# Batch norm behind a matmul: ten column units of the weight multiplied in strips of 32 columns

## The chip, the cores and the metric

The kernel runs on one core of a Trainium2 chip. TensorE multiplies: a weight load puts a stationary operand into its array, and a matmul then moves rows of the other operand past it, into a bank of PSUM. VectorE (DVE), ScalarE (ACT) and GpSimd (POOL) work on tiles in SBUF and PSUM; SyncE (SP) issues most of the stores. The time is that of one execution on the device in microseconds. Before the change it is 208.61 us, the median of two runs (208.1 and 209.12).

## The reference

```
batch, m, k, n = 16, 512, 1024, 768
y = np.matmul(x, weight)                       # x: (16, 512, 1024), weight: (1024, 768)
mean = np.mean(y, axis=(0, 1), keepdims=True)
var = np.var(y, axis=(0, 1), keepdims=True)
y_norm = (y - mean) / np.sqrt(var + eps)
return gamma * y_norm + beta
```

All is float32 outside; gamma is ones, beta zeros, eps 1e-5. The mean and the variance of a column are taken over all 8192 rows, so no column of the output can be written before its last row has been multiplied.

## The kernel before

The 8192 rows of x are cut into 16 chunks of 512 (index `c`), the 768 columns of the weight into 6 tiles of 128 (index `nt`). The contraction of 1024 runs in 8 steps of 128: four values of `jw`, two of `e`. x and the weight are cast to bf16 as they are loaded. A chunk of x is transposed by DVE into `xT_sb`. In most chunks two neighbouring values of the contraction stay side by side there, so a matmul reads its rows with a stride of two elements; in the chunks 2, 3 and 6 (`SINGLE`) they are apart. For the chunks 4, 5 and 7 to 10 (`PARTED`), and later 11 to 15 (`LATE`), a copy by ACT, POOL or DVE makes plain rows of them (`x_pl`).

The tiles 0 and 1 are multiplied with x stationary (`mm_rows`) while x is loaded. The tiles 2 to 5 follow with w stationary, one tile after the other: a *column unit* (`col_unit`, emitted by `mm`) is one tile and one chunk. It takes 8 pairs of a 128x128 weight load and a matmul of 512 moving rows, which all add up in one PSUM bank (128 columns of w as partitions, 512 rows of x as its row). A unit comes in two halves of 4 pairs (`halves`). Behind its second half `col_stats` takes the statistics of the bank (DVE, or ACT in the chunks 4 to 15 of tile 2) and ACT keeps the values as bf16 in `y_sb`. When a tile has all its 16 chunks, its scale and shift are worked out, its kept values are normalized, turned back and stored, while TensorE is at the next tile. The last tile has nothing behind it: its normalization, turning (`o_ps`, `o_sb`, L1028 and L1293) and stores make the end of the program. Turns of earlier tiles by TensorE can be taken in between the matmuls of a unit (`todo`).

The order on every engine is made by a planner (`arrange`): each piece of work is a `Task` with a due time, a cost for each engine that can do it, and what it needs. The planner knows a column unit by the cost that `col_unit` gives it (1.728 us for plain rows, 1.808 us for strided ones), not by the instructions that it emits.

Names that the prediction uses: L558 is the matmul of a column unit; L736 the units of the last chunk of the last tile, in two pieces of 256 rows; L493 the matmuls with x stationary (256 moving); L798 those of the last two chunks for the tiles 0 and 1 (256 moving); L577 a row of small matmuls at the start (128 moving); L855 eight passes in f32 with one row moving, that sum statistics over partitions; L1028 the turns of the end (128 moving). PSUM has 8 banks, taken in turn by all of these.

Of the kernel before, what the change touches and what calls it, by code (L numbers as in the profile page):

```python
# [227 lines left out]
def kernel(  # L228
# [9 lines left out]
    nc = tc.nc  # L238
# [9 lines left out]
    P = 128  # L248
    NT = N // P
    KQ = K // 4  # L250
    CH = 512
    RT = CH // P
    C = M // CH
    QR = 256
    QPC = CH // QR
    JW = KQ // 64
# [3 lines left out]
    SMALL = 22  # L260
    TOUCH = 1
    EARLY = 4
    SHORT = 2
    GA = 2
    NA = GA * P
# [4 lines left out]
    RC = C - 2  # L270
    XT, YB, SQ = C - EARLY, 28, 3
    ADDED = (0,6,16,28,40)
# [18 lines left out]
    def seq(bi):  # L291

        ins = bi.ins
        prev = last.get(ins.engine)
        if prev is not None:
            tc.add_manual_dep(
                ins, prev,
                mybir.DependencyInfo(mybir.DependencyClass.NoSync, mybir.DependencyReason.DATA),
                reason="order",
            )  # L300
        last[ins.engine] = ins.name
        return bi
# [7 lines left out]
    w_sb = singles.tile([P, JW, 2, N], bf16)  # L310
# [49 lines left out]
    def act(occ):  # L360
        return {"ACT": (occ, occ + 0.11)}
# [64 lines left out]
    order = [("x", 0), ("w", 0, 1)] + [("x", 1), ("w", 1, 2), ("w", 2, 4)]  # L426
    order += [("x", q) for q in range(2, SHORT * QPC)] + [("c", c) for c in range(SHORT, C - 1)]
    at = M - CH
# [5 lines left out]
    for kind, n, *n1 in order:  # L434
# [9 lines left out]
        rows = n1[0] if kind == "p" else QR if kind == "x" else CH  # L444
# [11 lines left out]
        for i in range(rows // QR):  # L456
            c, q = divmod(m0 // QR + i, QPC)
# [9 lines left out]
        if rows % QR:  # L467
            t0 = rows // QR * QR // 32
            m1 = m0 + 32 * t0
            c, q = divmod(m1 // QR, QPC)  # L470
# [8 lines left out]
    def x_of(c, jw, e, r0, r1):  # L479
        if c in SINGLE:  # L480
            return x_slot[c].tile[:, jw, e, r0:r1]
        return x_slot[c].tile[:, jw, r0:r1, e]
# [28 lines left out]
    def part_chunk(c, now, engines, small=False, step=0.0, after=()):  # L511

        src = x_slot[c]
        slots = [Slot(sqs if jw < SQ else ys) for jw in range(JW)] if small else [Slot(xts)] * JW
        ts = []

        def copy(jw):
            def emit(eng):
                if small:
                    if jw < SQ:  # L520
                        x_pl = sqpool.tile([P, 2, CH], bf16, tag="sq")
                    else:
                        x_pl = ypool.tile([P, 2, CH], bf16, tag="y")
                    slots[jw].tile = [x_pl]
                elif jw == 0:
                    x_pl = xtpool.tile([P, JW, 2, CH], bf16, tag="xT")
                    slots[0].tile = [x_pl[:, i] for i in range(JW)]
                dst = slots[jw].tile[0 if small else jw]
                pairs = src.tile[:, jw].rearrange("p m e -> p e m")
                seq(nc.scalar.copy(dst, pairs) if eng == "ACT" else ENG[eng].tensor_copy(dst, pairs))  # L530
            return emit

        for jw in range(JW):
            new = small or jw == 0
            ts.append(task(
                now + step * jw, engines, copy(jw), [x_ready[c, q, JW] for q in range(QPC)] + list(after) + ([] if new else ts[:1]),
                len(engines) > 1, uses=[src] + ([] if new else [slots[jw]]), takes=[slots[jw]] if new else []))
        plain[c] = slots, ts, small

    def moving(c, jw, e, r0, r1, parted):  # L540
        if parted:
            slots, _, small = parted
            return slots[jw].tile[0 if small else jw][:, e, r0:r1]
        return x_of(c, jw, e, r0, r1)

    def mm(nt, c, jws, slot, q0=0, q1=QPC):
        parted = plain.get(c)

        def emit(eng):
            if jws[0] == 0 and q0 == 0:  # L550
                y_ps = psum.tile([P, CH], f32, tag="b")
                slot.tile = y_ps
            y_ps = slot.tile[:, q0 * QR:q1 * QR]
            me = emit.task
            todo = [u for u, n in me.hosted for _ in range(n)]
            for jw in jws:
                for e in range(2):
                    seq(nc.tensor.matmul(  # L558
                        y_ps, w_sb[:, jw, e, nt * P:(nt + 1) * P],
                        moving(c, jw, e, q0 * QR, q1 * QR, parted),  # L560
                        start=(jw == 0 and e == 0 and q0 == 0), stop=(jw == JW - 1 and e == 1),
                        skip_group_check=True,
                    ))
                    if todo:
                        todo.pop(0).emit.step()
            while todo:
                todo.pop(0).emit.step()
        return emit
# [253 lines left out]
    for c in range(1, RC):  # L822
        for ts in ([0, 1], [2, 3]):
            rows_unit(c, ts)
        if c in PARTED:
            part_chunk(c, clock[0] + (4.0 if c < EARLY else 20.0), act(1.05))
        columns = ([c - 1] if 0 < c - 1 < EARLY and c - 1 in PARTED else []) + (
            [c] if c < EARLY and c not in PARTED else [])
        for c1 in columns:
# [372 lines left out]
    STEP = {2: 1.9, 3: 2.3, 4: 2.3}  # L1202
    CHUNKS = {nt: list(range(EARLY, C)) for nt in range(GA, NT)}
    if LATE:
        late = [c for c in range(EARLY, C) if c in LATE or c + 1 - c % 2 * 2 in LATE]
        rest = [c for c in range(EARLY, C) if c not in late]
        CHUNKS[NT - 3], CHUNKS[NT - 2] = late + rest, rest + late
    for nt in range(GA, NT - 1):
# [8 lines left out]
        start = clock[0] + 3.0  # L1217
# [12 lines left out]
    nt = NT - 1  # L1230
# [113 lines left out]
```

## Time and profile before

| | |
|---|---|
| median of the runs | 208.61 us (208.1 to 209.12) |
| span of the profiled execution, first to last instruction | 206.5 us |
| TensorE matmul busy | 191.4 us, 1211 instructions |
| TensorE weight load busy | 116.3 us, 1226 instructions |
| DVE, ACT, POOL busy | 156.3, 139.8, 132.0 us |
| L558 with x plain (`x_pl`) | 256 matmuls, 60.5 us |
| L558 with `xT_sb` | 241 matmuls, 55.1 us |
| last matmul of the last unit (L736) | 188.6 us |
| last stores issued by SP | 191.6 to 201.9 us |
| stores of 512 KB, from issue to landing | 3.7 us, median |

Times in the profile are in us from the first instruction, unless marked ns. PE stands for TensorE's matmuls, PEld for its weight loads. "L558" is line 558 of the kernel. The page cuts the span into 40 slices and gives for each the busy share of an engine in tenths, 9 for 90% or more; PEclk is the clock that TensorE was granted, in tenths of its full speed. The recorded time of a matmul reaches from its start to the modelled end of its results, so matmuls that follow each other closely overlap in the record: their pace is read from the distance of their starts. The chain of waits goes back from the last instruction to whatever released it, and names what the end of the program really hung on.

### The profile page before, as it was taken

Reading aid. Unit: us, or ns where it says so; the run is one execution under the profiler, and the core shown is the slowest. Engines: PE = TensorE matmul, PEld = TensorE weight load, DVE = VectorE, ACT = ScalarE, POOL = GpSimd, SP = SyncE. Lnnn points to the kernel's source line nnn. Section 1 sums busy time; section 2 is a strip of 40 time slices with the busy share of each in tenths; the row PEclk is TensorE's granted clock in tenths of the full one; section 3 lists DMA queues with packets and bytes.
Section 4 is the critical chain, followed back from the end, with each engine's and each line's share of the span. In section 5 each row is a group of like instructions: output and inputs, shape, how many; then the busy total and the mean of one; then the engine's idle time right before and its main releaser. Section 6 shows DMA issues by size and latency. Waiting matters only on the chain.

```text
span 206.5 us, 3506 instructions
## 1 busy us (share of the span) xinstructions
PE 191.4 (93%) x1211; PEld 116.3 (56%) x1226; DVE 156.3 (76%) x238; ACT 139.8 (68%) x248; POOL 132.0 (64%) x148
## 2 busy tenths in 40 slices
PE   7998999999999999999999999999999999996900
PEld 3465564747488888777875444444444445553600
DVE  4220779999999999968989998977999648947900
ACT  2000560369989999998978767997376776866950
POOL 7877964877488999999304999599954440440000
PEclk9999999999999999999999999999999999999995
DMA  5999999999999999999676898999999999999898
GB/s 55 169 168 193 192 196 196 196 198 197 190 193 197 197 197 195 196 197 195 110 120 199 311 339 307 267 350 307 315 317 245 291 325 308 274 341 347 254 347 243
DMA packets 98497, 48.73 MB, mean 236 GB/s; under 512 B 24240, under 2 KB 97968, under 8 KB 98480
## 3 DMA queue, kind: packets, MB, share of 16 engines
q0 software_dynamic: 34688, 18.36, 65.1%
q1 hardware_dynamic: 63792, 30.16, 52.8%
q8 instruction: 9, 0.15, 0.3%
q14 instruction: 8, 0.07, 0.1%
HBM read 36.71 MB, written 25.17 MB: 300 GB/s over the span
## 4 chain that ended last, share of the span: by engine, by line
PE 82%; DMA 8%; ACT 3%; issue 1%; POOL 1%; DVE 1%; ACTq 0%; POOLq 0%
PE y_ps L558 51%; PE y_ps L493 23%; DMA ring<-in_x_dram 5%; PE y_ps L798 4%; ACT o_sb L1293 3%; DMA w_sb<-in_weight_dram 3%; PE o_ps L1028 2%; PE a_ps L887 1%; POOL ring L392 1%; PE y_ps L736 1%; PE o_ps L1058 0%; ACTq L1339 0%; PE tot_ps L855 0%; DVE fin L743 0%; ACT y_sb L746 0%
## 5 line engine op out<-in xcount | busy, mean ns | idle before, releaser
L558 PEld LDWEIGHTS <-w_sb 128*128 128x128 bf16 x512 | 49.7, 97 | 57.4
L558 PE MATMUL y_ps<-x_pl,w_sb 128*128 128x512 bf16 x256 | 60.5, 379 | 0.3
L392 POOL DMA_DIRECT2D ring<-in_x_dram x76 | 47.5, 630 | 13.0 <-DVE xT_sb L414 5.0
L558 PE MATMUL y_ps<-xT_sb,w_sb 128*128 128x512 bf16 (+1 forms) x241 | 55.1, 376 | 0.4
L493 PE MATMUL y_ps<-w_sb,xT_sb 128*128 128x256 bf16 x448 | 50.7, 273 | 0.6 <-DMA w_sb<-in_weight_dram 0.6
L493 PEld LDWEIGHTS <-xT_sb 128*128 128x128 bf16 x448 | 43.6, 98 | 8.3 <-issue 1.7
L421 DVE STREAM_TRANSPOSE xT_sb<-ring 128x1024 f32<-128x1024 f32 (+1 forms) x29 | 31.2, 1111 | 12.4 <-DMA ring<-in_x_dram 12.2
L694 DVE BATCH_NORM_STATS2 stats<-y_ps 128x6 f32<-128x512 f32 x46 | 30.9, 687 | 12.7 <-PE y_ps L558 12.5
L698 ACT CAST y_sb<-y_ps 128x512 bf16<-128x512 f32 x51 | 29.4, 590 | 14.5 <-DVE stats L694 12.4
L926 POOL TENSOR_TENSOR ring<-ring,sum 128x1024 f32<-128x1024 f32 (+1 forms) x11 | 23.7, 2193 | 14.6 <-DVE ring L921 14.5
L649 POOL TENSOR_TENSOR sum<-sum,sq_sb 128x512 f32<-128x512 f32 x21 | 26.9, 1281 | 3.2 <-ACT sq_sb L642 2.1
L642 ACT ACTIVATE sq_sb<-y_ps 128x512 f32<-128x512 f32 x28 | 16.3, 607 | 18.0 <-PE y_ps L493 17.1
L645 DVE TENSOR_TENSOR sum<-y_ps,sum 128x512 f32<-128x512 f32 x28 | 18.9, 675 | 9.1 <-ACT sq_sb L642 7.8
L530 ACT COPY x_pl<-xT_sb 128x1024 bf16<-128x1024 bf16 x24 | 24.4, 1052 | 1.7 <-DVE xT_sb L421 1.7
L655 ACT CAST y_sb<-y_ps 128x512 bf16<-128x512 f32 x28 | 16.0, 599 | 7.8 <-DVE sum L645 7.6
L530 POOL COPY x_pl<-xT_sb 128x1024 bf16<-128x1024 bf16 x15 | 16.1, 1108 | 8.0 <-DVE x_pl L530 5.2
L921 DVE TENSOR_TENSOR ring<-y_sb,a_ps 128x1024 f32<-128x1024 bf16 (+1 forms) x16 | 16.7, 1080 | 0.3 <-DMA out_dram<-ring 0.3
L1139 POOL TENSOR_TENSOR ring<-ring,sum 128x1024 f32<-128x1024 f32 x4 | 9.6, 2412 | 11.0 <-DVE ring L1135 11.0
L1193 ACT CAST ring<-ring 128x1024 f32<-128x1024 bf16 x15 | 15.7, 1049 | 1.0 <-DMA ring<-y_sb 1.0
L1028 PE MATMUL o_ps<-ident,y_sb 128*128 128x128 bf16 x104 | 14.2, 221 | 2.2 <-DVE y_sb L1280 2.0
L414 DVE STREAM_TRANSPOSE xT_sb<-ring 128x2048 bf16<-128x2048 bf16 x6 | 13.5, 2289 | 0.2 <-DMA ring<-in_x_dram 0.2
L574 PE MATMUL idle_ps<-idle_sb 128*128 128x512 f32 x20 | 11.2, 717 | 1.5 <-DVE idle_sb L314 1.5
(97 smaller groups left out, 155.0 us busy)
## 6 DMA issues: line engine op xcount, KB each, us to landing
out_dram<-ring SPq DMA_DIRECT2D x38, 512.0 KB, 3.7
ring<-in_x_dram POOLq DMA_DIRECT2D x52, 256.0 KB, 8.8
out_dram<-o_sb SPq DMA_DIRECT2D x6, 512.0 KB, 4.9
ring<-in_x_dram POOLq DMA_DIRECT2D x16, 128.0 KB, 5.3
out_dram<-ring SPq DMA_DIRECT2D x4, 256.0 KB, 3.0
w_sb<-in_weight_dram POOLq DMA_DIRECT2D x8, 96.0 KB, 5.1
w_sb<-in_weight_dram POOLq DMA_DIRECT2D x4, 192.0 KB, 5.9
ring<-in_x_dram POOLq DMA_DIRECT2D x4, 192.0 KB, 8.1
```

The lines of the kernel that those rows point to most:

```text
L392: bi = seq(nc.gpsimd.dma_start(x_bf[32 * i:32 * i + 32], src[:, :, KQ * i:KQ * (i + 1)]))
L421: seq(nc.vector.transpose(dst, src[:, :, jw0:jw1]))
L493: seq(nc.tensor.matmul(y_ps[:, s], x_of(c, jw, e, t * P, (t + 1) * P), w_sb[:, jw, e, 0:NA], start=(s == 0 and jw == 0 and e == 0), stop=( ...
L530: seq(nc.scalar.copy(dst, pairs) if eng == "ACT" else ENG[eng].tensor_copy(dst, pairs))
L558: seq(nc.tensor.matmul(y_ps, w_sb[:, jw, e, nt * P:(nt + 1) * P], moving(c, jw, e, q0 * QR, q1 * QR, parted), start=(jw == 0 and e == 0 an ...
L645: seq(nc.vector.tensor_add(sum1, slot.tile[:, 0:n], sum1))
L649: seq(ENG[eng].tensor_add(acc, acc, state["sq"][:, 0:n]))
L694: seq(nc.vector.bn_stats(dst, slot.tile))
L698: seq(nc.scalar.copy(y(nt, c), slot.tile))
L921: seq(nc.vector.tensor_mul(slot.o, y_row[c].y[:, s0:s1], aff[0][:, None, :].to_broadcast([P, n, NA])))
L926: seq(ENG[eng].tensor_add(slot.o, slot.o, row[:, None, :].to_broadcast([P, n, NA])))
L1028: seq(nc.tensor.transpose(dst, src, ident))
```

## The change

A table names ten pairs of tile and chunk. For these, a step's weight load and matmul are cut along the columns of w into four strips of 32, each into its own 32 partitions of the bank. The 512 rows are cut as well, into pieces of 512, 256, 128 or 64 rows as the table says (1, 2, 4 or 8 pieces). In each turn of the inner loops the four strips are at different pieces: the strip `n0 // wide` takes the piece `(i + n0 // wide) % parts`. With one piece all four strips have the same 512 rows. Every strip matmul has a weight load of its own. All other units take the same path with one strip of 128 and one piece of 512 rows (256 in the first chunk), and are as before.

```diff
     EARLY = 4
+    STRIPS = {(2, 12): (32, 512), (2, 13): (32, 512), (3, 8): (32, 128), (3, 9): (32, 128), (3, 10): (32, 128),
+              (4, 4): (32, 256), (4, 5): (32, 256), (4, 6): (32, 256), (5, 4): (32, 64), (5, 5): (32, 64)}
     SHORT = 2
...
             for jw in jws:
                 for e in range(2):
-                    seq(nc.tensor.matmul(
-                        y_ps, w_sb[:, jw, e, nt * P:(nt + 1) * P],
-                        moving(c, jw, e, q0 * QR, q1 * QR, parted),
-                        start=(jw == 0 and e == 0 and q0 == 0), stop=(jw == JW - 1 and e == 1),
-                        skip_group_check=True,
-                    ))
+                    wide, long = STRIPS.get((nt, c), (P, CH))
+                    rows = moving(c, jw, e, q0 * QR, q1 * QR, parted)
+                    parts = max((q1 - q0) * QR // long, 1)
+                    long = (q1 - q0) * QR // parts
+                    for i in range(parts):
+                        for n0 in range(0, P, wide):
+                            r0 = (i + n0 // wide) % parts * long
+                            seq(nc.tensor.matmul(
+                                y_ps[n0:n0 + wide, r0:r0 + long], w_sb[:, jw, e, nt * P + n0:nt * P + n0 + wide],
+                                rows[:, r0:r0 + long],
+                                start=(jw == 0 and e == 0 and q0 == 0 and i == 0),
+                                stop=(jw == JW - 1 and e == 1),
+                                skip_group_check=True,
+                            ))
                     if todo:
                         todo.pop(0).emit.step()
```

The two units of tile 2 read `xT_sb` with its stride, the unit (4, 6) reads `xT_sb` of a `SINGLE` chunk, and the other seven read `x_pl`.

## The prediction

> **What bounds the kernel now.** I read the page first: its busy shares, its slices and its chain of waits.
>
> ```profile
> span 206.5 us, 3506 instructions
> ...
> PE 191.4 (93%) x1211; PEld 116.3 (56%) x1226; DVE 156.3 (76%) x238; ACT 139.8 (68%) x248; POOL 132.0 (64%) x148
> ...
> PE   7998999999999999999999999999999999996900
> ...
> PEclk9999999999999999999999999999999999999995
> ...
> PE 82%; DMA 8%; ACT 3%; issue 1%; POOL 1%; DVE 1%; ACTq 0%; POOLq 0%
> ```
>
> TensorE is full in every slice from the fifth to the thirty-sixth, at the full clock, and 82% of the chain is its own. The waits listed for it are three, 4.1 us together, at the start and in the tail: between 21 and 188 us it waits for nobody. An added TensorE microsecond there is a microsecond at the end, and a saved one is saved. So the question is what the ten units cost TensorE.
>
> Next I matched the weight loads of the two programs in order with those of the trace (one load per bf16 matmul, so they can be counted), to find when the ten units run, and asked for the busy time of those stretches.
>
> ```profile
> 115.40:119.00 3.60, 3.60 (x18) 1.53 (x16) 3.57 (x5) 2.58 (x8) 3.60 (x2) 1.00 0.79 280
> 122.70:124.40 1.70, 1.70 (x9) 0.78 (x8) 1.70 (x2) 1.28 (x5) 1.70 (x2) 1.00 1.09 386
> 140.80:144.20 3.40, 3.40 (x17) 1.57 (x16) 2.38 (x4) 2.30 (x5) 3.40 (x3) 1.00 1.15 316
> 144.20:149.40 5.20, 5.15 (x25) 2.35 (x24) 4.69 (x9) 2.38 (x5) 4.71 (x5) 1.00 1.14 304
> 163.20:165.80 2.60, 2.60 (x14) 1.18 (x12) 1.45 (x3) 1.46 (x3) 2.04 (x3) 1.00 1.20 326
> 166.70:167.50 0.80, 0.80 (x5) 0.39 (x4) 0.00 (x0) 0.80 (x2) 0.80 (x2) 1.00 1.27 288
> ```
>
> The columns after the length are PE, its weight loads, DVE, ACT and POOL, then the clock and the DMA. The units are the two with 512 rows moving (first line), the three with 128 (second and third), the three with 256 (fourth) and the two with 64 (last two, with an untouched half unit between). PE is full in all six. The third number says that 16 loads and 16 matmuls take 3.60 us: 225 ns a step where x is read with a stride, and 24 in 5.20, 216 ns, where it is plain.
>
> Last, what a matmul and a load cost when they are small, from the chain and from PE's timelines (the group lines end in busy us and mean ns):
>
> ```profile
> 185.31 1.73 PE y_ps L558 x8
> 187.04 1.83 PE y_ps L736 x16
> ```
>
> ```profile
> L558 PE MATMUL y_ps<-x_pl,w_sb 128*128 128x512 bf16 x256 | 60.5, 379 | 0.3
> L558 PEld LDWEIGHTS <-w_sb 128*128 128x128 bf16 x512 | 49.7, 97 | 57.4
> ```
>
> ```profile
> 10.67 1.39 PE L577 MATMUL idle_ps<-idle_sb 128*128 128x128 bf16 x22
> ```
>
> ```profile
> 100.38 0.97 PEld L855 LDWEIGHTS tot_ps<-ones,tot 128*128 128x128 f32 x8
> ```
>
> ```profile
> 194.38 0.11 PEld L1028 LDWEIGHTS <-y_sb 128*128 128x128 bf16 x2
> ```
>
> A matmul lasts 379 ns but the next begins 1.73/8 = 216 ns after it: 163 ns of each lie under the next, and its 97 ns load is hidden too. With 256 rows the step is 1.83/16 = 114 ns strided (32 matmuls of L493 take 3.49 us in the chain: 109 plain). With 128 rows, 22 steps end at 1.39 us, the last lasting 219 ns: (1390 - 219)/21 = 56 ns, load included. L855 has one row moving, so only its loads count: (970 - 192)/7 = 111 ns per load of 128 columns, 0.87 ns a column. In the last line two loads end at 0.11 us and one alone takes 0.10: the shortest distance of two loads is 10 to 15 ns.
>
> **The change, part by part.** Each step (a pair jw, e: 16, 24, 24 and 16 steps in the four sorts) was one load and one 512-row matmul. It becomes 4, 8, 16 or 32 pairs of a 32-column load and a matmul: 64 pairs with 512 rows, 192 with 256, 384 with 128, 512 with 64, 1152 in all for 80. The program's TensorE order grows from 2375 rows to 4519; the orders of DVE, ACT, POOL and SP are the same row for row, and nothing is planned anew, since the units' cost in the planner is untouched. That the change does not do what it says is thus excluded. Removed: 80 x 216 ns, 17.3 us by the six lines.
>
> *Streaming.* If the four strips stream side by side, four pairs pass the same rows in the time in which the full array passed them once, and streaming costs what it did. There is no gain in it: no path below 216 ns a step is to be seen, since the array was full. No row shows a strip. The nearest is the 163 ns overlap of two matmuls in one array, which is for side by side; the bound on the other side is one after the other (first rival).
>
> *Loads.* A pair cannot go faster than its load. From below the bound is 15 ns (L1028's two loads), from above 56 ns (a whole 128-row pair). I take L855, where loads alone set the pace, by columns: 32 x 0.87 = 28 ns. One round of four pairs is then 112 ns at least.
> - 512 rows: 112 is under 225. 0.
> - 256 rows: 192 x 28 = 5.38, less 24 x 216 = 5.18: 0.2 us.
> - 128 rows: 384 x 28 = 10.75, less 5.18: 5.6 us.
> - 64 rows: 512 x 28 = 14.34, less 16 x 216 = 3.46: 10.9 us.
> Sum 16.7 us. At 15 ns the same four terms are 0, 0, 0.6 and 4.2: 4.8 us. At 56 ns they are 0, 5.6, 16.3 and 25.2: 47.1 us.
>
> *Borders.* The units stand in five groups, so TensorE changes ten times between the full array and strips. If a change let the array run empty, it would cost the 163 ns that otherwise lie under the next matmul, 1.6 us in all; if not, nothing. Neither end has a row of a change of shape, so I take the middle, 0.8 us.
> The Trainium skill speaks here ("TensorEngine Tiling (Array Packing)", Key Properties): a change of tiling mode drains TensorE. By it the term is 1.6 us and the time 226.9; by the row of L855, at whose edges the 256-row matmuls keep their pace though the loads change kind, it would be 0 and 225.3. No run here shows it yet.
>
> *What lies behind.* Later matmuls wait longer in PE's queue, so their inputs are only earlier; the evictions by DVE and ACT move with them. Stores: the last one before the tail is issued by 188.9 us and takes 3.7 us to land, the tail's first at 191.6, so at most 1 us of backlog could be won back with stores pausing. I take 0. Code: the page has 9 instruction packets, 0.15 MB, on TensorE's queue, 264 rows each. At 28 ns a pair one is needed every 3.7 us, where it was some 25 us; they hold an engine for 1.1 us (0.3% of 16 x 206.5 us, by 9). That is hidden if the next packet is asked for a packet ahead, and if landing takes no longer than a store's 3.7 us; at 5.3 us, the row for the smaller x loads, a pair would take 40 ns: 2.5 + 10.2 + 17.0 = 29.7 us.
>
> Sum: 206.5 of the profiled span + 16.7 + 0.8 = 224.0, and 2.1 us that the median of 208.61 lies above that span: 226.1 us.
>
> **Rivals.**
> *Strips one after the other.* Each matmul then holds the array for its own stream: 512 rows: 16 x 3 x 225 = 10.8 us; 256: 24 x (8 x 109 - 216) = 15.7; 128: 24 x (16 x 56 - 216) = 16.3; 64: 16 x (32 x 28 - 216) = 10.9. Sum 53.7, time 263. For it: no row has two matmuls streaming at once, and the 512-row units are its sign, as loads cannot slow them. Against it: array parts free at different times are used already (the 163 ns).
> On this alone the skill has a measurement ("TensorE: Matmul & The Clock Gate", Measured speedup vs the span model): three column strips with 512 rows ran 2.38 times faster than in turn. No run here shows that yet; by it the time is the forecast's and not 263.
>
> *Pairs slower than their load.* Loads and matmuls may each need a turn at issue, or code may come late; the pair lies between 33 and 56 ns. At 40 ns: 208.6 + 29.7 + 0.8 = 239; at 56: 256.5. For it: no pair faster than 56 ns stands in this trace. Against it: those have 128 rows, which explains 56 by itself.
>
> *Pairs faster than the slow load,* 15 to 25 ns: at 20 ns 0 + 0 + 2.5 + 6.8 = 9.3, time 218.7. For it: the 10 to 15 ns of L1028.
>
> *Not slower: the four strips load side by side.* If each strip takes its weights by its own way, a round of four needs one load, 28 ns, and 64-row streaming needs 28 too. Nothing but borders is added: 208.6 to 210.2. The point that decides is 14 ns a pair: under it 128 rows cost nothing and 64 rows under 512 x 14.3 - 3.46 = 3.9 us. For it: a 128-column bf16 load takes 97 ns and an f32 one 192, so some loads do go in parallel. Against it: pairs are queued in one order, and 15 ns is the shortest distance seen.
>
> **How the numbers follow.** Forecast, 25 to 33 ns a pair (13.8 to 22.1 us, 222 to 232): 0.48. Faster pairs, 213 to 222: 0.15. Slower pairs, 232 to 257: 0.18. One after the other, 263: 0.13. Side by side: 0.05. A remainder of 0.01 for a gain that I can't name. From 214 to 252 I leave out side by side and the gain (0.06), the serial case (0.13) and about 0.01 on either edge. 2% of 208.61, 4.2 us, is about what a measurement tells from no change: faster 0.01, within 2% 0.06, slower 0.93.
>
> **What would show it.** In the changed profile the 512-row units should still take 3.6 us and the 256-row ones 5.2 to 5.5; the 128-row ones some 10.8, the 64-row ones some 14.3, with weight loads 28 ns apart and the clock at 1.00. If the 512-row units take four times as long, strips don't overlap, and the first step is wrong. If the 64-row units take 3.5 us, the load is not the bound. If pairs are regular but slower than 28 ns, the load or issue is mis-sized; if they come in bursts of about 264 rows with pauses, code is late; a clock under 1 would undo all terms. Behind 168 us the trace should be the old one, moved.

## The result, and the profile after

The changed kernel takes 225.83 us (225.78 and 225.88) against 208.61: 1.0837 times as long, 95% interval 1.0781 to 1.0893. The forecast was 226.1. The total agrees almost to the microsecond, by luck: the profile shows that it is made of other parts than the forecast's. The largest term of the sum, the loads, did not happen as described, and two causes that were set at nothing took its place.

The page of the changed kernel, with the lines that answer to those of before:

```profile
span 224.0 us, 5666 instructions
...
PE 200.3 (89%) x2298; PEld 129.8 (58%) x2298; DVE 154.2 (69%) x238; ACT 139.8 (62%) x248; POOL 132.1 (59%) x148
...
PE   7999999999999999999999999669996499996900
...
PEclk9999999999999999999999999988999559999665
...
q8 instruction: 18, 0.29, 0.5%
...
PE 88%; issue 4%; ACT 3%; DVE 1%; ACTq 0%
```

TensorE is still the chain, but it is no longer full: two notches in its row of slices, at the 26th and 27th slice and at the 31st and 32nd, and two in its clock, right behind them. In the chain "issue", time in which TensorE waited for nothing that the profile shows, went from 1% to 4%. The instruction packets on TensorE's queue went from 9 to 18.

The stretches of the ten units, with the columns as before (length, PE, its loads, DVE, ACT, POOL, clock, DMA):

```profile
115.15:118.95 3.80, 3.80 (x65) 1.71 (x65) 3.77 (x4) 2.58 (x8) 3.80 (x3) 1.00 0.81 284
122.67:124.57 1.90, 1.90 (x129) 1.79 (x129) 1.76 (x2) 1.77 (x9) 1.72 (x2) 1.00 1.09 381
141.06:146.59 5.53, 3.77 (x256) 3.59 (x259) 2.63 (x4) 3.06 (x4) 4.88 (x3) 1.00 1.12 312
146.59:153.98 7.39, 5.34 (x142) 4.61 (x134) 2.95 (x8) 1.35 (x3) 3.70 (x4) 0.77 1.19 259
153.98:155.93 1.95, 1.95 (x75) 1.74 (x64) 1.63 (x3) 0.90 (x2) 0.19 (x1) 1.00 0.88 146
169.85:179.98 10.13, 4.97 (x386) 4.60 (x385) 1.40 (x2) 3.06 (x4) 3.99 (x4) 0.70 0.73 170
181.79:183.75 1.96, 1.96 (x129) 1.80 (x129) 0.00 (x0) 0.00 (x0) 0.00 (x0) 0.50 0.53 89
```

The 512-row units take 3.80 us (3.60 before). The first 128-row unit takes 1.90 us for 128 pairs, 14.9 ns a pair, where the forecast's 28 ns a pair would be 3.6. The other two, one behind the other, take 5.53 us, but TensorE is busy for 3.77 of it. So with the first two 256-row units (5.34 of 7.39; the third, in the fifth line, is full) and the first three quarters of the 64-row pairs (4.97 of 10.13). The time is lost in holes, not in the pairs. The waits of TensorE name them:

```profile
PE y_ps L567 <- issue: 9.0, 4, 3.3
```

and its timeline has the four (start, length, what follows, idle before it):

```profile
145.34 2.50 PE L567 MATMUL y_ps<-x_pl,w_sb 128*32 128x128 bf16 x128 [1.76 <-issue]
149.90 4.36 PE L567 MATMUL y_ps<-x_pl,w_sb 128*32 128x256 bf16 x91 [2.05 <-issue]
...
174.90 1.90 PE L567 MATMUL y_ps<-x_pl,w_sb 128*32 128x64 bf16 x128 [3.33 <-issue]
178.63 5.19 PE L567 MATMUL y_ps<-x_pl,w_sb 128*32 128x64 bf16 x223 [1.83 <-issue]
```

If TensorE's loads and matmuls of the trace are counted from the start, the work goes on behind the four holes at the numbers 2471, 2727, 3495 and 3751: multiples of 256 apart. On TensorE's instruction queue a packet finishes moving 1.26 to 1.33 us before each of the four restarts (144.08, 148.59, 173.64, 177.30 us). It looks as if TensorE had run out of program: the program comes in packets of 256 rows (one row is one load or one matmul), and a strip unit uses up a packet faster than the next one comes.

How fast a strip unit is when it has its code is seen at the start of the 64-row group:

```profile
169.85:171.37 1.52, 1.52 (x165) 1.49 (x165) 0.70 (x1) 0.68 (x2) 1.33 (x2) 1.00 1.15 339
174.90:176.55 1.65, 1.65 (x126) 1.65 (x128) 0.20 (x1) 0.00 (x0) 0.00 (x0) 0.50 1.03 172
149.90:153.35 3.45, 3.45 (x68) 2.97 (x71) 1.66 (x6) 0.59 (x1) 0.39 (x1) 0.51 1.17 329
```

165 pairs in 1.52 us are 9.2 ns a pair. In the trace four loads and four matmuls start within 10 ns, and the next four 29 ns later: 64 rows, streamed once, by four strips at a time. Only the first ten such rounds keep this pace. Behind them the matmuls start one by one, 8.3 ns apart, in the two units alone and in the first half of the run with four halves apart (both below) as here; what sets that pace is not shown. The second line is the same work at half clock (13 ns a pair), the third the 256-row strips at half clock: 51 ns a pair where eight pairs in 216 ns would be 27.

My theory from this profile: strips cost nothing in themselves but a border (a change between strips and the full array) of 0.1 us; what costs is **late code**, a packet of 256 rows that is not there in time, and the half clock that such holes bring. Its rival is the prediction's **slow load**, 28 ns for each pair wherever it stands.

### The profile page after: what moved, and what is told of

It is laid out like the page before. It is cut to its first block, busy times and chain, and to the rows that moved or that the text cites. A ratio compares the mean times of both kernels' runs of the same rounds, so it can differ in the third digit from the quotient of the medians.

```text
span 224.0 us, 5666 instructions
## 1 busy us (share of the span) xinstructions
PE 200.3 (89%) x2298; PEld 129.8 (58%) x2298; DVE 154.2 (69%) x238; ACT 139.8 (62%) x248; POOL 132.1 (59%) x148
## 4 chain that ended last, share of the span: by engine, by line
PE 88%; issue 4%; ACT 3%; DVE 1%; ACTq 0%
PE y_ps L567 53%; PE y_ps L495 22%; PE idle_ps L584 5%; PE y_ps L808 3%; ACT o_sb L1303 2%; PE o_ps L1038 2%; PE a_ps L897 1%; PE y_ps L746 1%; PE idle_ps L587 1%; PE o_ps L1068 0%; ACTq L1349 0%; PE tot_ps L865 0%; DVE idle_sb L316 0%; DVE fin L753 0%; ACT y_sb L756 0%
## 5 line engine op out<-in xcount | busy, mean ns | idle before, releaser
L567 PEld LDWEIGHTS <-w_sb 128*32 128x32 bf16 (+1 forms) x1584 | 61.4, 106 | 62.4 <-issue 13.7
L567 PE MATMUL y_ps<-x_pl,w_sb 128*32 128x64 bf16 (+3 forms) x1232 | 68.2, 263 | 9.0 <-issue 9.0
L567 PE MATMUL y_ps<-xT_sb,w_sb 128*128 128x512 bf16 (+3 forms) x352 | 56.4, 360 | 0.0
L936 POOL TENSOR_TENSOR ring<-ring,sum 128x1024 f32<-128x1024 f32 (+1 forms) x11 | 23.9, 2201 | 15.0 <-DVE ring L931 14.9
L652 ACT ACTIVATE sq_sb<-y_ps 128x512 f32<-128x512 f32 x28 | 16.3, 607 | 17.6 <-PE y_ps L495 17.2
```

Of the source, the lines that this page charges most:

```text
L567: seq(nc.tensor.matmul(y_ps[n0:n0 + wide, r0:r0 + long], w_sb[:, jw, e, nt * P + n0:nt * P + n0 + wide], rows[:, r0:r0 + long], start=(jw ...
L936: seq(ENG[eng].tensor_add(slot.o, slot.o, row[:, None, :].to_broadcast([P, n, NA])))
```

## The experiments

All are changes of the table of strips, if nothing else is said; where its key has a third number, that is the first `jw` of a half unit (0 or 2). Times over before are the ratio, less one, times the median of the runs of before beside it, with the 95% interval.

**The same 64-row pairs, together and apart.** First the two 64-row units of the change alone:

```diff
-    STRIPS = {(2, 12): (32, 512), (2, 13): (32, 512), (3, 8): (32, 128), (3, 9): (32, 128), (3, 10): (32, 128),
-              (4, 4): (32, 256), (4, 5): (32, 256), (4, 6): (32, 256), (5, 4): (32, 64), (5, 5): (32, 64)}
+    STRIPS = {(5, 4): (32, 64), (5, 5): (32, 64)}
```

> Only the two units with 64 rows moving are in strips (512 pairs, side by side in the program); all else is the kernel before. Slow load (the prediction's step: 28 ns a pair wherever it stands): 512 x 28 - 3.46 = 10.9 us and 4 borders, 11.3 us over before. Late code (a pair costs some 9 ns, as the first 165 of the changed kernel's 64-row pairs did, but TensorE's program comes in packets of 256 rows, one in 3.7 us at best, and a pause of 2 us or more brings half clock): what these units and the matmuls right behind them cost in the changed kernel, about 9.7 us over before, with two pauses and a stretch of half clock. These two are too near each other here; this run is the base for the next.

Then the same 512 pairs in four half units with whole ones between them:

```diff
+    STRIPS = {(5, 4, 0): (32, 64), (5, 6, 0): (32, 64), (5, 8, 0): (32, 64), (5, 10, 0): (32, 64)}
...
-                    wide, long = STRIPS.get((nt, c), (P, CH))
+                    wide, long = STRIPS.get((nt, c, jws[0]), (P, CH))
```

> The same 512 strip pairs with 64 rows, but as four half units (128 pairs each) with three untouched half units (2.6 us, few rows of code) or more between them. Slow load: it does not matter where the pairs stand, 10.9 us and 8 borders of 0.1, about 11.7 us over before. Late code: 256 rows fit into what is already fetched, and the next packet has 2.6 us more; 4 x (128 x 9.2 ns - 0.865 us) = 1.2 us and 8 borders of 0.1, about 2 us over before, no pause above 0.5 us and the clock at 1.00 throughout.

Together they take 11.0 us over before (10.1 to 11.9), apart 3.0 (2.4 to 3.6). The slow load, 11.3 and 11.7, would do for the first alone, but not for both: it falls. Together the waits of TensorE show 7.7 us of issue, in the longest hole 3.7:

```profile
PE y_ps L566 <- issue: 7.7, 5, 3.7
```

and behind it 10.24 us of half clock. Apart, three of the halves, with the same columns as above:

```profile
163.31:164.70 1.39, 1.23 (x130) 1.23 (x131) 0.70 (x1) 0.54 (x2) 1.19 (x2) 1.00 1.17 332
168.03:169.89 1.86, 1.31 (x130) 1.16 (x129) 0.70 (x1) 0.59 (x1) 0.00 (x0) 1.00 0.67 169
173.45:174.84 1.39, 1.30 (x129) 1.15 (x128) 1.39 (x3) 0.96 (x2) 0.00 (x0) 1.00 1.31 100
```

A half unit of 128 pairs takes 1.39 us with its borders (0.87 whole), the second 1.86 with a hole of 0.55 in it; the clock stays. The 3.0 us were expected as 2.

**Nearer together.**

```diff
+    STRIPS = {(5, 4, 0): (32, 64), (5, 5, 0): (32, 64), (5, 6, 0): (32, 64), (5, 7, 0): (32, 64)}
```

> The 512 strip pairs with 64 rows in four half units again, with only one or two untouched half units (0.9 to 1.7 us) between them. Slow load: 11.7 us over before, as everywhere. Late code: 256 rows are used up in 2.2 to 3.0 us where a packet took 3.7 to 5 in the runs so far, so pauses of 1 to 2.5 us come back, at the second or third half: between the 3.0 us of the halves far apart and the 11.0 us of the two units together, about 6 us.

8.4 us over before (7.3 to 9.5), with 4.6 us of issue in three holes and no half clock before the tail. The direction is late code's, and the place matters a third time; the size, some 6 us, was too small.

**All pairs of the change, apart.** The same number of pairs of each sort, in other units:

```diff
+    STRIPS = {(2, 12): (32, 512), (2, 13): (32, 512), (3, 10): (32, 128), (3, 4): (32, 128), (3, 8): (32, 128),
+              (4, 6): (32, 256), (4, 8): (32, 256), (4, 10): (32, 256),
+              (5, 4, 0): (32, 64), (5, 6, 0): (32, 64), (5, 8, 0): (32, 64), (5, 10, 0): (32, 64)}
```

> As many strip pairs of each sort as in the change (64 with 512 rows, 192 with 256, 384 with 128, 512 with 64), in other units: between two groups of them stand whole units or half units, so that 256 rows of TensorE's code last longer. Slow load (28 ns a pair) or any cost of a pair by itself: place does not matter, about 17 us over before, as in the change. Late code: the 64-row pairs 3.0 us as in the run with four halves apart, the 128-row ones 3 x 0.17 (as the unit (3, 10) in the change), the 256- and 512-row ones a border at either end, 8 x 0.11: about 4.5 us over before, no pause above 1 us, no half clock before the tail.

9.8 us over before (8.7 to 11.0): well under the change's 17.5, but twice what I expected, and with a hole of almost 3 us behind the third 64-row half:

```profile
177.56 0.38 PE L568 MATMUL y_ps<-x_pl,w_sb 128*128 128x512 bf16 x1
180.82 1.04 PE L568 MATMUL y_ps<-x_pl,w_sb 128*128 128x512 bf16 x4 [2.88 <-issue]
```

The 256 rows of the half before it, but for ten, are one packet, counted in rows from the other holes: it was begun at 175.88 us and used up at 177.56, and the next was ready at 180.82. Distance alone was too simple a rule; what counts is how many of the fast rows fall into one packet. That can be tested without moving any pair.

**The packets shifted against the work.** To this kernel, and to the one with four halves apart, 176 weight loads without a matmul are added far ahead, in tile 2, where whole matmuls of 216 ns hide them. All later packets then begin 176 rows earlier in the work:

```diff
+    PADS = {(2, c): 4 if c < 7 else 2 for c in range(4, 12)}
...
                 for e in range(2):
+                    for i in range(PADS.get((nt, c), 0)):
+                        seq(nc.tensor.ldweights(w_sb[:, jw, e, i % 2 * P:(i % 2 + 1) * P]))
```

> The run with the same pairs apart, and 176 weight loads without a matmul added in the units 4 to 11 of tile 2, where a matmul of 216 ns hides them: no pair changes, but every later packet of 256 rows of TensorE's code begins 176 rows earlier in the work. In the run without them one packet coincided with the 256 rows of a half unit (it began 10 rows before them) and a pause of 3.26 us stood behind it, beside one of 0.41. Late code: now the packets begin 96 to 166 rows into the 64-row halves, no packet is used up in under 3.7 us, so no pause above 0.6 us and some 3 us less than without the shift: 6 to 7.5 us over before. A pause that belongs to the pairs or to their place in the program: it stays, 10 us over before.

> The run with four halves apart and the same 176 loads. There the packets began 84 rows before the second half and 115 before the third, and the pauses were 0.75 and 0.38 us. Shifted, a packet begins 4 rows before the second half's 256 rows. Late code: these are used up in 1.6 us, so a pause of 2 to 3.3 us comes up behind them, and the time is 2 to 3 us longer than without the shift: 5 to 6 us over before, or more if the clock falls. No effect of where packets begin: 3 us over before, as without.

> The control: the kernel before with the same 176 loads. Both theories: the loads are hidden, 0 to 0.5 us over before. If they cost more (176 x 28 ns is 4.9 us), the other two runs have to be read against this.

The control is 0.25 us over before (-0.1 to 0.6): the loads are hidden. With them the pairs apart take 6.9 us over before (6.5 to 7.4) and not 9.8, and the hole is gone:

```profile
176.71 0.49 PE L901 MATMUL a_ps<-ident,scale 128*128 128x128 f32 x2
177.03 0.39 PE L901 MATMUL a_ps<-ident,shift 128*128 128x128 f32 x2
177.47 1.03 PE L571 MATMUL y_ps<-x_pl,w_sb 128*128 128x512 bf16 x4
```

The same loads make the four halves apart slower, 4.0 us over before (3.6 to 4.4) where it was 3.0 (2.4 to 3.6). These two intervals touch, so the times alone do not settle it; the trace does, with a hole exactly where the shifted packet ends, two pairs before the end of the second half:

```profile
168.17 1.21 PE L569 MATMUL y_ps<-xT_sb,w_sb 128*32 128x64 bf16 x126
170.62 0.21 PE L569 MATMUL y_ps<-xT_sb,w_sb 128*32 128x64 bf16 x2 [1.25 <-issue]
```

It was 1.25 us where I had expected 2 to 3.3: this packet came 3.0 us after the one before it was begun (167.64 to 170.62), faster than any other. One and the same edit, which costs nothing alone, takes a hole away in one kernel and makes one in the other: the holes belong to the packets, not to the strips.

**Full-width matmuls that use as much code.**

```diff
+    STRIPS = {(5, c): (128, 32) for c in range(4, 8)}
```

> No strips: four units of the last tile in full-width matmuls of 32 moving rows, 16 pairs a step, 512 pairs, so as many rows of code as two strip units of 64 rows. Pauses belong to the strip mode: none here, only the pair's own pace (16 ns by streaming, 25 ns if a pair cannot go faster): 1.3 to 5.9 us over before. Late code: at 16 ns 256 rows last 2.0 us, at 25 ns 3.2, under the 3.7 to 5 of a packet, so there are pauses without strips too, three or four of 0.5 to 3 us: 6 to 11 us over before.

8.2 us over before (7.2 to 9.2). The first 192 pairs take 4.80 us, 25.0 ns each, so 512 cost 5.9 us; the rest has holes that no strip is near:

```profile
175.41 1.02 PE L566 MATMUL y_ps<-xT_sb,w_sb 128*128 128x32 bf16 x34 [0.97 <-issue]
...
179.14 1.89 PE L566 MATMUL y_ps<-x_pl,w_sb 128*128 128x32 bf16 x38 [0.36 <-issue]
```

They are 256 rows apart again. At 25 ns a pair a packet lasts 3.2 us, so they are short: two holes with 1.3 us, where I had expected three or four.

**Borders, and strips with much to stream.** All ten units with 512 rows, and then strips in every second step of six units (here the third number of the key is `e`):

```diff
+    STRIPS = {(2, 12): (32, 512), (2, 13): (32, 512), (3, 8): (32, 512), (3, 9): (32, 512), (3, 10): (32, 512),
+              (4, 4): (32, 512), (4, 5): (32, 512), (4, 6): (32, 512), (5, 4): (32, 512), (5, 5): (32, 512)}
```

> The same ten units in the same strips of 32 columns, all with 512 rows moving: 320 pairs. Strips one after the other: 10 units x 3 x 1.73 us, 52 us over before. Slow load and late code both: four loads (112 ns) under 216 ns, and 256 rows of code in 6.9 us, so nothing but the ten borders, at 0.1 us each 1 us over before, and none or 163 ns each as the ends (0 to 1.6 us).

```diff
+    STRIPS = {(4, c, 0): (32, 512) for c in range(4, 10)}
...
+                    wide, long = STRIPS.get((nt, c, e), (P, CH))
```

> In six units every second step is in strips with 512 rows and the step between is whole: 96 strip pairs and 48 borders between strips and the full array. A border empties the array: 48 x 163 ns = 7.8 us over before. A border costs what the starts in the changed trace show (0.31 us from the last full matmul to the first strip where 0.22 is usual): 48 x 0.1 = 4.8 us. A border is free: under 0.3 us.

The ten units take 1.7 us over before (1.1 to 2.3), 50 us less than in turn: the four strips stream at once. (I had expected 1 us; in the profile 0.5 us of it lies behind TensorE's last unit.) The 48 borders take 5.5 us (4.7 to 6.2), and their stretch, with 47 borders inside it,

```profile
144.29:159.61 15.32, 14.56 (x117) 4.66 (x119) 10.04 (x18) 7.09 (x11) 7.49 (x6) 1.00 1.13 275
```

is 4.9 us longer than 48 whole steps (10.40 us from 143.60 to 154.00 in the kernel before): 0.10 us a border. It is neither free nor the whole 163 ns.

**The 256-row units alone.**

```diff
+    STRIPS = {(4, 4): (32, 256), (4, 5): (32, 256), (4, 6): (32, 256)}
```

> Only the three units with 256 rows are in strips: 192 pairs. In the change they cost 4.2 us, with a pause of 2.05 us and half clock behind it. If that belongs to 256 rows: 4 us over before here too. Slow load: 0.2 us and two borders. Late code: 256 rows of code last 3.46 us, just under a packet's 3.7, and the code before them is thin, so at most a short pause: 0.2 to 1 us over before.

3.0 us over before (2.1 to 3.9), more than I expected: there is one hole of 1.2 us of issue, two pairs before the end, and no half clock before the tail. A packet used up in 3.46 us is thus too fast already. Of the rest 1.2 us lie behind the last unit of TensorE, see below.

**The same rows for all four strips,** in the run with four halves apart:

```diff
-                            r0 = (i + n0 // wide) % parts * long
+                            r0 = i * long
```

> The run with four halves apart, with the four strips of a round on the same 64 rows of x instead of four different pieces (the sums are the same, in another order of pieces). If the strips read their rows independently: no difference, 3.0 us over before. If one stream can serve four strips only when they want the same rows, or if four readers of the same rows disturb each other: the 64-row rounds change from 29 ns, by up to 4 x 32 x (4 x 28 - 29) ns = 10 us the one way; the other way there is only 2 us to win.

3.1 us over before (2.2 to 4.0), against 3.0 on different rows (2.4 to 3.6): that part of the change makes no difference that shows here.

## Why the prediction came true, and where it failed

- *What bounds.* Right. The seven stretches and the half unit among them are 16.3 us longer than the same work before, and the program 17.5. Another 1.4 us lie behind TensorE's last unit, in the tail, and TensorE came to the first stretch 0.25 us earlier than before.
- *Streaming.* Right: no gain, and with 512 and 128 rows no loss but the borders; four strips share the time of one pass.
- *Loads.* This is the step that failed: "A pair cannot go faster than its load ... 28 ns". Read from loads of the full array, it was carried over to strips by columns. The four strips load side by side: four pairs in 29 ns at first, and 8.3 ns a pair after ten rounds. By this term the three 128-row units should have taken 10.8 us, and took 7.4; the 64-row units 14.3, and took 12.1; the 256-row units 5.4, and took 9.3. The sum came out by luck, one term being too large and others missing: the loads were given 16.7 us, and of the 16.3 measured only 2.5 are left for them when holes, half clock and borders (below) are taken off. The rival "side by side" had the loads right and the time wrong, for it too left out the code.
- *Code.* Set at nothing, on the condition that the next packet is asked for in time and lands in 3.7 us. It failed: from the start of one packet to the moment that the next can be used, the runs show 3.0 to 5.3 us (2.98 in the shifted four halves, 3.73 and 4.56 in the change, 4.94 in the pairs apart, 5.10 in the two units alone, 5.33 in the four halves apart), and strips use up a packet in 1.2 (64 rows) to 3.5 us (256 rows). Four holes, 9.0 us of the 16.3. The prediction had named late code beside its rival of slower pairs, and its sign under "What would show it": "bursts of about 264 rows with pauses". That sign is what the profile shows, but with pairs faster than 28 ns.
- *The clock.* Held for constant. Behind the holes it was halved from 149.9 to 153.4 us and from 173.8 to 184.1. By the paces above this cost some 1.6 us in the 256-row strips (68 pairs, 24 ns each), 0.9 in the four whole matmuls that start 0.43 us apart around 181 us, and 1.3 in the 64-row pairs (347, some 4 ns each): 3.8 us. That is worked out from the trace; no run separates it from the holes. The Trainium skill ("TensorE: Matmul & The Clock Gate", Part 1: The HAM clock gate) has a free-running window of 3.4 us after which an idle TensorE goes to half clock. The stretches here are 3.41 and 10.24 us long, one window and three, as it says. But a window need not be idle throughout. If the traces are cut into windows of 3.41 us, laid back from the changes of the clock, the half clocks of the change and of the two units follow windows with 2.05, 2.26 and 2.60 us of idle TensorE, while the hole of 2.88 us in the pairs apart falls on two windows, 1.32 and 1.56 us, and brings none, nor does the hole of 1.76 us in the change. Over all runs, from 100 us on, each full-clock window with at least 2.04 us idle is followed by half clock, and of those with at most 1.92 us only one is (1.4 us, in the tail of the shifted four halves). No run was made to test this.
- *Borders.* 0.8 us taken, 10 x 0.10 by the run with 48 of them. The skill ("TensorEngine Tiling (Array Packing)", Key Properties) has a drain at a change of mode. A cost is there, two thirds of what a full drain would be by the 163 ns; that it is a drain is not shown.
- *What is left.* Holes 9.0, half clock 3.8, borders 1.0 and the 64-row pairs' 9.2 ns against 6.8 by streaming (216 ns for 32 pairs; 512 x 2.4 ns, 1.2 us) are 15.0 of the 16.3 us; the rest are waits under half a microsecond. The tail is 1.4 us longer in the change, and 1.2 to 1.5 longer in the 256-row units alone and the pairs apart, with the last stores issued later, but eight of the other runs are within 0.2 us of before there (the ten units with 512 rows are 0.5 longer, the pairs apart with the loads 0.9). In the three runs with the longest tails and in no other a packet of TensorE's program moves while the last stores run (209.64 to 211.07 us in the change). That this holds the stores up is not shown, and the cause stays open.

No version here beats the kernel before: the strips can at best do the same streaming in the same time, and they pay for borders and code.

## What to carry to other kernels

Count the rows of code, not only the time of the work: here TensorE's program came late where it used up 256 rows in less than the 3.0 to 5.3 us that the next packet took, and the profile shows it as "issue" in front of ordinary work, at multiples of 256 rows. A forecast that comes out right in the total can be wrong in its terms; compare each stretch with its own number before trusting it, and change the place of the suspected work without changing its amount, which separates a price per piece from a supply that runs dry. A price measured with the full array (28 ns per 32 columns) need not hold for its parts.

## What the runs showed of the hardware that was not expected

- Four column strips load and stream at once, with starts 2 to 5 ns apart; the first ten 64-row rounds of four pairs follow each other in 29 ns, and then the pairs start one by one, 8.3 ns apart. The skill ("TensorE: Matmul & The Clock Gate", Wait — 56ns, not 53.3ns?) has a floor of about 25 ns between starts of matmuls. The full-width pairs with 32 rows keep to it, at 25.0 ns; strips don't, with four starts in 29 ns.
- In all 16 holes of at least 0.36 us in these runs, TensorE goes on 1.26 to 1.52 us after a packet of its program has finished moving.
- A border between strips and the full array costs 0.10 us (4.92 us for 47, with 512 rows).
- Four strips on the same rows of x and on different ones take the same time (3.1 and 3.0 us over before, with 64 rows).
